# An encoder layer in split float32: the low parts of weights and modulated rows made by VectorE alone

## The chip, the cores and the metric

The kernel runs on one core of one Trainium2 chip. The metric is the device time of one execution in microseconds, and of several executions the median. The engines are TensorE (PE, with its weight loads as PEld), VectorE (DVE), ScalarE (ACT), GpSimd (POOL) and SyncE (SP, which here only issues DMAs).

## The reference

One encoder layer is computed for two independent sequences of 512 rows and 1024 columns (b = 0 and b = 1 below), with the same weights, all in float32:

```python
mod = silu(c) @ w_ada + b_ada                 # six vectors: sh1, sc1, g1, sh2, sc2, g2
h = rms_norm(x, norm1_g) * (1 + sc1) + sh1
q_a, k_a, v_a, q_r, k_r, v_r, g_r = split(h @ w_in)
o_a = windowed_attention(q_a, k_a, v_a, sink)  # 8 heads, 2 key heads, |t - s| <= 128, ALiBi, a sink logit
o_r = bidirectional_retention(q_r, k_r, v_r, g_r)   # 4 heads of 128, forward and backward decay, gated
x = x + g1 * (concat(o_a, o_r) @ w_out)
h = rms_norm(x, norm2_g) * (1 + sc2) + sh2
x = x + g2 * (square(relu(h @ w_mlp1)) @ w_mlp2)
y = rms_norm(x, final_g)
```

w_in has 2816 columns (512 q_a, 128 k_a, 128 v_a, and four times 512 for q_r, k_r, v_r, g_r), w_mlp1 4096.

## The kernel before, in words

**Split products.** To keep float32 accuracy with TensorE's faster format (fp32r), each operand is split in a high part (a cast to fp32r, made by ScalarE) and a low part (the operand less its high part, a subtraction). A product is then three matmuls (`mm3`, lines 128 to 130): high x high, high x low, low x high. A low part is needed for the second or third of these only, so a little later than the high part. Names: `raw_..` is a weight as loaded, `wh_..` and `wl_..` are its high and low part; the suffix says which: rv (the retention's values, four units of 256 rows of the weight), rq, rk, rg (retention queries, keys and gates, one unit for each head), wo (the output projection, eight units). `h` is a modulated, transposed row block of the normed input, with both parts in one tile, `hm` the same before the split.

**The sequence.** The front (to about 75 us) makes the modulation of the first norm and the first six column blocks of the input projection for sequence 0. Then sequence 0's retention projections run unit by unit, mixed with its attention blocks (names `psc` scores, `st` scores after the bias, `negm` and `den` softmax statistics, `ppt` and `pt` transposed weights, `po` outputs; the two digits behind a name are the head group and the block of 128 queries) and then with its retention heads (`prs`, `rsf`, `rsc` scores, `py` and `ryt` output, `pyn`, `ryn`, `pyb` the per-head norm, `dtab` the decay table). From 175 us `norm_x1` loads, norms (`rv_x`, `rr_x`, `x`) and modulates the rows of sequence 1, and the same projections follow for it, from the split weights that sequence 0 has stored in DRAM (`keep_unit`, `kept_unit`): there no weight is split again. From about 415 us the output projection of sequence 0 runs with its own splits, then that of sequence 1 from the stored ones, and from about 520 us the MLP, in a scheme of seven products instead of eight. Beside all this, `ada_gate` and `ada_columns` build the other modulation vectors as running sums on VectorE (`adacc_g`, `adacc_c`), four units of weights each; the gates are written to DRAM by a DMA that GpSimd issues (`gates`).

**What sets the order.** A unit's `load` (a load on SP into `raw`, the cast on ACT, the subtraction) is issued one unit ahead of its use, and `between` mixes steps of attention, retention, norm and background into the matmuls. The order that comes out is then a scheduler's, engine by engine; at run time each engine works through its list strictly in that order and waits on semaphores. In the front the order is pinned as written; behind it, moving an instruction to another engine also moves others. SP's list has, for each unit of sequence 0, the stores of its high and low part, each of which waits for its part, and the load of a later unit behind them. `raw` has three buffers, the split weights four (two units).

**Who made the low parts.** In the front they are shared between DVE and GpSimd. Behind the front GpSimd makes those of all weight units (line 103 of `split_unit`, with `lo_engine`) and those of `h` for the odd column blocks of sequence 1 (line 328); DVE makes the rest: those of `h` for even blocks, of scores, transposed weights, projections and mixed outputs. GpSimd also computes the powers of the norms (`rr_x` line 306, `rrs` line 485) and issues the gates' stores (line 292).

Of the kernel before, what the change touches and what calls it, by code (L numbers as in the profile page):

```python
# [15 lines left out]
P = 128  # L16
# [3 lines left out]
KC = D // P  # L20
# [10 lines left out]
def trunk_kernel(ctx, tc, x0, x1, c0, c1, w_ada, b_ada, norm1_g, w_in, attn_sink, decay_f, decay_b,  # L31
                 w_out, norm2_g, w_mlp1, w_mlp2, final_g, y0, y1):
    nc = tc.nc
    xin = (x0[0], x1[0])
    yout = (y0[0], y1[0])
    w_ada, b_ada, w_in, w_out = w_ada[0], b_ada[0], w_in[0], w_out[0]
# [12 lines left out]
    def mm_bank(name):  # L49
        return psum.tile([P, 512], F32, tag="mm", name=name, bufs=3)  # L50
# [4 lines left out]
    def r4(name, dtype=F32R):  # L55
        return work.tile([P, 2, 512], dtype, tag="r4", name=name, bufs=N_R4)
# [4 lines left out]
    def f2(name, dtype=F32):  # L61
        return work.tile([P, 512], dtype, tag="f2", name=name, bufs=8)
# [7 lines left out]
    def f(ap):  # L70
        return ap.bitcast(F32)
# [14 lines left out]
    def raw_unit(src, name, spare=False):  # L86
        t = r4f(f"raw_{name}") if spare else work.tile([P, 1024], F32, tag="raw", name=f"raw_{name}", bufs=3)
        n = src.shape[1] * src.shape[2]
        nc.sync.dma_start(t[:, :n].rearrange("p (a n) -> p a n", n=src.shape[2]), src)
        return t  # L90

    def split_high(t, name, pool=None):
        if pool is spare_ws:
            w = [r4(f"w{s}_{name}").rearrange("p a n -> p (a n)") for s in "hl"]
        else:
            w = [(pool or work).tile([P, 1024], F32R, tag="ws", name=f"w{s}_{name}", bufs=4) for s in "hl"]
        nc.scalar.copy(w[0], t)
        return w

    def split_unit(src, name, lo_engine, pool=None):  # L100
        t = raw_unit(src, name)
        w = split_high(t, name, pool)
        lo_engine.tensor_sub(w[1], t, f(w[0]))  # L103
        return [x.rearrange("p (a n) -> p a n", n=src.shape[2]) for x in w]
# [4 lines left out]
    def keep_unit(key, w):  # L109
        d = kept[key] = tc.dram_tile((P, 2, 1024), F32, name=f"kept_{key}")  # L110
        for s in range(2):
            nc.sync.dma_start(d[:, s, :], f(w[s]).rearrange("p a n -> p (a n)"))

    def kept_unit(key, name, n, lows=None):
        w = []
        for s in range(2):
            pool, tag, bufs = ((work, "ws", 4), lows or (work, "raw", 3))[s]
            t = pool.tile([P, 1024], F32R, tag=tag, name=f"w{'hl'[s]}_{name}", bufs=bufs)
            nc.sync.dma_start(f(t), kept[key][:, s, :])
            w.append(t.rearrange("p (a n) -> p a n", n=n))  # L120
        return w

    def cols_unit(wt, k0, nk, col, n):
        return wt[k0 * P:(k0 + nk) * P, col:col + n].rearrange("(k p) n -> p k n", p=P)

    def mm3(ps, lhs, rhs, start, stop):

        nc.tensor.matmul(ps, lhs[0], rhs[0], start=start, stop=False)  # L128
        nc.tensor.matmul(ps, lhs[0], rhs[1], start=False, stop=False)  # L129
        nc.tensor.matmul(ps, lhs[1], rhs[0], start=False, stop=stop)  # L130
# [192 lines left out]
    def modulated(which, b, kc, src):  # L323
        dst = r4(f"h_{which}_{b}_{kc}")
        t = f2(f"hm_{which}_{b}_{kc}")
        nc.vector.tensor_scalar(t, src, mod_a[which][:, kc, b:b + 1], mod_s[which][:, kc, b:b + 1], ALU.mult, ALU.add)
        nc.scalar.copy(dst[:, 0, :], t)
        (nc.vector if kc % 2 == 0 or which == b == 0 else nc.gpsimd).tensor_sub(dst[:, 1, :], t, f(dst[:, 0, :]))
        return dst

    def split2(ps_, name):
# [305 lines left out]
    def proj_unit(hT, col, name, done):  # L637
        key = f"in{col}"

        def load():  # L640
            if hT is hT_of[1]:
                return kept_unit(key, name, P)
            return split_unit(cols_unit(w_in, 0, KC, col, P), name, nc.gpsimd)

        def use(w):
            bank = mm_bank(f"pj_{name}")
            for k in range(KC):
                mm3(bank, (w[0][:, k, :], w[1][:, k, :]), (hT[k][:, 0, :], hT[k][:, 1, :]), k == 0, k == KC - 1)
                if k == 3:
                    yield  # L650
            done(bank)
            yield
        return Unit(load, use, done, None if hT is hT_of[1] else lambda w: keep_unit(key, w))
# [34 lines left out]
    def ret_v_units(hT, b):  # L688

        banks = []  # L690

        def unit(kq):
            key = f"rv{kq}"

            def load():
                if b == 1:
                    return kept_unit(key, f"rv{b}_{kq}", 512)
                return split_unit(cols_unit(w_in, kq * 2, 2, 1792, 512), f"rv{b}_{kq}", nc.gpsimd)

            def use(w):  # L700
                if kq == 0:
                    banks.extend((mm_bank if t < 3 else aux_bank)(f"pj_rv{b}_{t}") for t in range(NT))
                for t in range(NT):
                    tsl = slice(t * P, (t + 1) * P)
                    for k in range(2):
                        kk = kq * 2 + k
                        mm3(banks[t], (hT[kk][:, 0, tsl], hT[kk][:, 1, tsl]), (w[0][:, k, :], w[1][:, k, :]),
                            kk == 0, kk == KC - 1)
                    if kq == 3:
                        ret_v[b].append(split2(banks[t], f"rv_{b}_{t}"))  # L710
                    if t == 1:
                        yield
                yield
            return Unit(load, use, None, (lambda w: keep_unit(key, w)) if b == 0 else None)
        return [unit(kq) for kq in range(4)]
# [20 lines left out]
    def out_units(b, late=None):  # L736
# [10 lines left out]
        def unit(hf, kq):  # L747
            hs = slice(hf * 512, (hf + 1) * 512)

            key = f"wo{hf}_{kq}"  # L750

            def load():
                if b == 1:
                    w = kept_unit(key, f"wo{b}_{hf}_{kq}", 512, (late, "ws2", 3))
                else:
                    w = split_unit(cols_unit(w_out, kq * 2, 2, hf * 512, 512), f"wo{b}_{hf}_{kq}", nc.gpsimd)
                if hf == 0:
                    ms = halves[kq] = []
                    for k in range(2):
                        m_ = r4(f"ms_{b}_{kq}_{k}")  # L760
                        nc.scalar.copy(m_[:, 0, :], mix[kq][:, k, :])  # L761
                        nc.vector.tensor_sub(m_[:, 1, :], mix[kq][:, k, :], f(m_[:, 0, :]))
                        ms.append(m_)
                if kq == 2:
                    gr[hf] = gate_row(0, b, hs)
                return w, halves[kq]

            def use(wm):
                w, ms = wm
                if kq == 0:  # L770
                    banks[hf] = [(mm_bank if t < 3 else aux_bank)(f"po_{b}_{hf}_{t}") for t in range(NT)]
                for t in range(NT):
                    tsl = slice(t * P, (t + 1) * P)
                    for k in range(2):
                        kk = kq * 2 + k
                        mm3(banks[hf][t], (ms[k][:, 0, tsl], ms[k][:, 1, tsl]), (w[0][:, k, :], w[1][:, k, :]),
                            kk == 0, kk == KC - 1)
                    if t == 1:
                        yield
                if kq == 3:  # L780
                    for t in range(NT):
                        if hf == 0:
                            x2[t] = x2_tile(t)
                            tc.keep_in_program_order(nc.sync.dma_start(x2[t], xin[b][t * P:(t + 1) * P, :]))
                        g_ = f2(f"go_{b}_{hf}_{t}")
                        nc.vector.tensor_tensor(g_, banks[hf][t], gr[hf], ALU.mult)
                        nc.vector.tensor_tensor(x2[t][:, hs], x2[t][:, hs], g_, ALU.add)

                    def squares():
                        for t in range(NT):  # L790
                            nc.scalar.activation(junk(f"jk2_{b}_{hf}_{t}")[:, :512], x2[t][:, hs], AF.Square,
                                                 accum_out=ss[t][:, hf:hf + 1])
                    if hf == 0:
                        later.append((clock[0] + 2, squares))
                    else:
                        halves["squares"] = squares
                yield
            return Unit(load, use, None, (lambda wm: keep_unit(key, wm[0])) if b == 0 else None)

        def norm2():  # L800
# [677 lines left out]
```

## Time and profile before

| | us |
|---|---|
| median of three runs | 1181.89 |
| the three runs | 1181.77 to 1184.57 |
| the profiled execution | 1184.46 |
| its span in the trace | 1182.7 |
| PE, DVE, ACT, POOL busy in it | 1117.8, 933.6, 493.9, 133.4 |

The profiled execution is 2.6 us above the median, and 1.8 us of it lie outside the span that the trace shows. Times in the trace are counted from the span's start. A matmul's recorded duration includes its way through the array, so consecutive ones overlap. "PEclk" is the share of full speed that TensorE's clock was granted. In the views, `out<-in` names what an instruction writes and reads, "x" how many of them; in a wait, the name ahead of the arrow waits for the one behind it, with the us in total, the times, and the longest.

### The profile page before, as it was taken

How to read it: one execution, taken by the hardware profiler on the slowest of the kernel's cores; microseconds unless marked ns; L12 is line 12 of the kernel's file. 1: busy time of each engine (PE TensorE's matmuls, PEld its weight loads, DVE VectorE, ACT ScalarE, POOL GpSimd, SP SyncE). 2: the span in 40 equal slices, each digit the busy share in tenths (PEclk: the TensorE clock that was granted, in tenths of full speed). 3: DMA queues.
4: the chain of work that ended last, by engine and by line, in shares of the span. 5: the costliest groups of instructions: out<-in, count | busy, mean ns of one | idle time of the engine just before them, and what ended most of it. 6: DMA issues, size and time to landing. Idle time of an engine off the chain costs nothing.

```text
span 1182.7 us, 14508 instructions
## 1 busy us (share of the span) xinstructions
PE 1117.8 (95%) x5167; PEld 909.0 (77%) x5167; DVE 933.6 (79%) x1522; ACT 493.9 (42%) x846; POOL 133.4 (11%) x107
## 2 busy tenths in 40 slices
PE   5889899999999999999999999999999999999975
PEld 3667777777888878888878888888778888888854
DVE  4887978877887687598998778886686876968896
ACT  4446665433745234246333333333444432432341
POOL 3632223301000033100000000000000000000012
PEclk9999999989999999999999999999999999999988
DMA  9786557554545578951655455542767264363513
GB/s 286 232 270 222 194 186 264 198 198 160 184 160 174 179 257 325 334 186 62 208 175 179 156 175 188 166 160 98 259 221 266 80 200 147 123 215 126 195 36 142
DMA packets 124112, 224.36 MB, mean 190 GB/s; under 512 B 8501, under 2 KB 59781, under 8 KB 124041
## 3 DMA queue, kind: packets, MB, share of 16 engines
q1 hardware_dynamic: 111144, 217.14, 54.9%
q10 hardware_dynamic: 12544, 6.29, 1.8%
q8 instruction: 40, 0.66, 0.2%
q0 software_dynamic: 352, 0.03, 0.1%
q14 instruction: 32, 0.25, 0.1%
HBM read 152.36 MB, written 71.06 MB: 189 GB/s over the span
## 4 chain that ended last, share of the span: by engine, by line
PE 69%; DVE 12%; DMA 4%; issue 3%; ACT 3%; POOL 2%; DVEq 0%; POOLq 0%; ACTq 0%; SPq 0%
PE px_None L936 13%; PE x L1310 12%; PE py_None L936 9%; PE y L1310 9%; PE po L129 2%; PE po L128 2%; PE po L130 2%; PE ppt L422 1%; PE po L429 1%; DVE adacc_g L255 1%; DMA raw_ada_c<-in_w_ada_dram 1%; PE psc L396 1%; PE pj_rk L128 1%; PE pj_rk L130 1%; PE pj_rg L130 1%
## 5 line engine op out<-in xcount | busy, mean ns | idle before, releaser
L841 ACT CAST uc_0h<-ur 128x1024 fp32r<-128x1024 f32 x28 | 29.4, 1052 | 68.7 <-PE x L1310 38.1
L1310 PE MATMUL x<-wc_0l,uc_0h 128*128 128x512 f32 x128 | 51.0, 398 | 5.4 <-DVE wc_0l L842 5.4
L1310 PE MATMUL x<-wc_0h,uc_0h 128*128 128x512 f32 x128 | 50.8, 398 | 3.9 <-DVE acc L1356 3.2
L128 PE MATMUL po<-wh_wo,ms 128*128 128x512 f32 x128 | 51.0, 398 | 2.6 <-ACT ms L761 2.0
L1310 PE MATMUL x<-wc_1h,uc_1h 128*128 128x512 f32 x128 | 50.5, 396 | 2.3 <-ACT wc_1h L841 2.3
L129 PE MATMUL po<-wl_wo,ms 128*128 128x512 f32 x128 | 50.5, 395 | 0.7 <-POOL wl_wo L103 0.7
L1310 PE MATMUL x<-wc_1l,uc_1h 128*128 128x512 f32 x128 | 50.5, 394 | 0.5 <-DVE wc_1l L842 0.5
L1310 PE MATMUL x<-wc_0h,uc_0l 128*128 128x512 f32 x128 | 50.5, 395 | 0.0
L1310 PE MATMUL x<-wc_1h,uc_1l 128*128 128x512 f32 x128 | 50.5, 395 | 0.0
L842 DVE TENSOR_TENSOR uc_0l<-ur,uc_0h 128x1024 fp32r<-128x1024 f32 x28 | 34.2, 1221 | 20.1 <-ACT uc_0h L841 16.3
L130 PE MATMUL po<-wh_wo,ms 128*128 128x512 f32 x128 | 49.4, 390 | 0.0
L255 DVE SCALAR_TENSOR_TENSOR adacc_c<-raw_ada_c,cact,adacc_c 128x512 f32<-128x512 f32 x56 | 42.9, 800 | 7.2 <-DMA raw_ada_c<-in_w_ada_dram 6.2
L406 ACT ACTIVATE st<-st,negm 128x256 f32<-128x256 f32 (+1 forms) x64 | 35.2, 555 | 20.3 <-DVE negm L401 20.2
L841 ACT CAST wc_0h<-w 128x1024 fp32r<-128x1024 f32 x24 | 25.2, 1049 | 43.6 <-DVE w L1289 17.6
L841 ACT CAST wc_s4h<-raw_w 128x1024 fp32r<-128x1024 f32 x16 | 16.8, 1052 | 62.6 <-PE px_None L936 41.6
L255 DVE SCALAR_TENSOR_TENSOR adacc_g<-raw_ada_g,cact,adacc_g 128x512 f32<-128x512 f32 x56 | 42.2, 784 | 0.4 <-ACT adacc_g L253 0.3
L1365 POOL TENSOR_SCALAR msf<-ssf 128x1 f32<-128x1 f32 x8 | 4.3, 540 | 336.0 <-ACT jkf L1362 335.9
L842 DVE TENSOR_TENSOR wc_0l<-w,wc_0h 128x1024 fp32r<-128x1024 f32 x24 | 29.3, 1221 | 13.5 <-ACT wc_0h L841 13.4
L936 PE MATMUL py_None<-hch,wc_a 128*128 128x512 f32 x120 | 39.7, 390 | 0.1
L936 PE MATMUL px_None<-hch,wc_a 128*128 128x512 f32 x120 | 39.5, 390 | 0.0
L936 PE MATMUL px_None<-hch,wc_s 128*128 128x512 f32 x120 | 39.4, 389 | 0.0
L1310 PE MATMUL y<-wc_1l,uc_1h 128*128 128x512 f32 x96 | 37.5, 390 | 0.6 <-DVE wc_1l L842 0.6
(398 smaller groups left out, 3583.4 us busy)
## 6 DMA issues: line engine op xcount, KB each, us to landing
ur<-spill SPq DMA_DIRECT2D x56, 512.0 KB, 4.2
raw_w<-in_w_mlp_dram SPq DMA_DIRECT2D x32, 512.0 KB, 4.3
spill<-s SPq DMA_DIRECT2D x64, 256.0 KB, 4.2
w<-in_w_mlp_dram SPq DMA_DIRECT2D x32, 512.0 KB, 5.8
spill<-u SPq DMA_DIRECT2D x48, 256.0 KB, 2.3
raw_ada_g<-in_w_ada_dram SPq DMA_DIRECT2D x16, 512.0 KB, 4.4
raw_ada_c<-in_w_ada_dram SPq DMA_DIRECT2D x16, 512.0 KB, 4.2
raw_ada<-in_w_ada_dram SPq DMA_DIRECT2D x12, 512.0 KB, 8.9
```

The source lines that it names most:

```text
L128: nc.tensor.matmul(ps, lhs[0], rhs[0], start=start, stop=False)
L129: nc.tensor.matmul(ps, lhs[0], rhs[1], start=False, stop=False)
L130: nc.tensor.matmul(ps, lhs[1], rhs[0], start=False, stop=stop)
L255: nc.vector.scalar_tensor_tensor(acc[b], src, cb, acc[b], ALU.mult, ALU.add)
L396: nc.tensor.matmul(psc[:, :w], qs[hh][:, isl], k_[:, s, j0 * P:j1 * P], start=(s == 0), stop=(s == 1))
L406: nc.scalar.activation(st[hh][:, :w], st[hh][:, :w], AF.Exp, bias=negm[:, hh:hh + 1], scale=0.125, accum_out=den[:, hh:hh + 1])
L422: nc.tensor.transpose(pt[:, hh * P:(hh + 1) * P], st[hh][:, jj * P:(jj + 1) * P], ident)
L429: nc.tensor.matmul(po, va[:, j0 + jj, g].rearrange("p s e -> p (s e)"), pts[jj][:, s, :], start=(jj == 0 and s == 0), stop=(jj == nj - 1 a ...
L841: nc.scalar.copy(hi, src)
L842: nc.vector.tensor_sub(lo, src, f(hi))
L936: self.last = nc.tensor.matmul(bank[:, cs], x[:, k, :], y, start=first and k == 0 and i == 0, stop=last and k == 3 and i == 2, skip_group_ ...
L1310: nc.tensor.matmul(out, u[x][:, i % 2, ts_], w[y][:, i % 2, :], start=first and i == 0 and k == 0, stop=end and i == GP - 1 and k == 2, sk ...
```

## The change

All low parts that GpSimd made behind the front are made by VectorE: the operand `lo_engine` of three calls of `split_unit` is `nc.vector`, and the condition on line 328 goes. These are 4 rv, 12 rq, rk and rg, and 8 wo units of 128x1024, and four `h` of 128x512. GpSimd keeps the norms' powers and the gates' stores, and its share of the pinned front.

```diff
@@ def modulated
         nc.scalar.copy(dst[:, 0, :], t)
-        (nc.vector if kc % 2 == 0 or which == b == 0 else nc.gpsimd).tensor_sub(dst[:, 1, :], t, f(dst[:, 0, :]))
+        nc.vector.tensor_sub(dst[:, 1, :], t, f(dst[:, 0, :]))
@@ def proj_unit
-            return split_unit(cols_unit(w_in, 0, KC, col, P), name, nc.gpsimd)
+            return split_unit(cols_unit(w_in, 0, KC, col, P), name, nc.vector)
@@ def ret_v_units
-                return split_unit(cols_unit(w_in, kq * 2, 2, 1792, 512), f"rv{b}_{kq}", nc.gpsimd)
+                return split_unit(cols_unit(w_in, kq * 2, 2, 1792, 512), f"rv{b}_{kq}", nc.vector)
@@ def out_units
-                    w = split_unit(cols_unit(w_out, kq * 2, 2, hf * 512, 512), f"wo{b}_{hf}_{kq}", nc.gpsimd)
+                    w = split_unit(cols_unit(w_out, kq * 2, 2, hf * 512, 512), f"wo{b}_{hf}_{kq}", nc.vector)
```

The scheduler puts the moved subtractions into DVE's list and reorders around them; from the MLP on the lists are the same. Three places follow, each a piece of the difference (- before, + now).

On DVE, at the softmax of head group 0's last block (at about 127 us; `pt` are transposed weights of the block before, `adacc_g` running sums, `den` and `rden` the block's denominators):

```order
 L334 TENSOR_TENSOR pt_0_2_2_1248<-ppt_0_2_2_1243,pt_0_2_2_1248 128x512
-L255 SCALAR_TENSOR_TENSOR adacc_g_0_0_1054<-raw_ada_g_0_2_1459,cact,adacc_g_0_0_1054 128x512
+L255 SCALAR_TENSOR_TENSOR adacc_g_0_1_1055<-raw_ada_g_0_1_1251,cact,adacc_g_0_1_1055 128x512
+L103 TENSOR_TENSOR wl_rk_0_1260<-raw_rk_0_1257,wh_rk_0_1259 128x1024
 L409 TENSOR_TENSOR den_0_3_1196<-den_0_3_1196,es_0_3_1194 128x4
-L255 SCALAR_TENSOR_TENSOR adacc_g_0_1_1055<-raw_ada_g_0_2_1459,cact,adacc_g_0_1_1055 128x512
+L437 TENSOR_TENSOR mix_0_807<-po_0_2_1279,otmp_0_2_1286 64x2x128
 L411 RECIPROCAL rden_0_3_1203<-den_0_3_1196 128x4
```

The low part of the first key unit now stands ahead of the denominators, and two running sums of the next weights have moved further down.

On DVE, where the rows of sequence 1 are normed (at about 183 us; `rv_x` is the input of the power on GpSimd, `x` the scaled rows, `dl` and `dtab` the decay table of head 1):

```order
 L286 TENSOR_TENSOR adsp_0_0_1_1830<-adacc_g_0_0_1054,adsp_0_0_0_1829 128x512
+L103 TENSOR_TENSOR wl_rg_2_1942<-raw_rg_2_1939,wh_rg_2_1941 128x1024
 L304 TENSOR_SCALAR rv_x_0_1866<-ssq_0_1863 128x1
+L559 TENSOR_SCALAR dl_0_1_1895<-dl,nlb 128x896
 L321 TENSOR_SCALAR x_0_1855<-x_0_1855,rr_x_0_1868 128x1024
-L559 TENSOR_SCALAR dl_0_1_1895<-dl,nlb 128x896
+L304 TENSOR_SCALAR rv_x_1_1874<-ssq_1_1871 128x1
 L561 TENSOR_TENSOR dtab_1_1896<-dtab_1_1896,dl_0_1_1895 128x896
-L304 TENSOR_SCALAR rv_x_1_1874<-ssq_1_1871 128x1
 L321 TENSOR_SCALAR x_1_1857<-x_1_1857,rr_x_1_1876 128x1024
```

A gate unit's low part now stands ahead of the first tile's statistics, and the second tile's `rv_x` ahead of `dtab` instead of behind it.

On POOL, from the power of the last tile of sequence 1 to that of the first retention head's norm (190 to 213 us):

```order
 L306 TENSOR_TENSOR rr_x_3_1892<-rv_x_3_1890,neghalf 128x1
-L103 TENSOR_TENSOR wl_rq_3_2033<-raw_rq_3_2030,wh_rq_3_2032 128x1024
-L328 TENSOR_TENSOR h_1_1_2003<-hm_1_1_2004,h_1_1_2003 128x512
 L292 DMA gates<-adacc_g_0_0_1054 16x1x32
-L103 TENSOR_TENSOR wl_rk_3_2123<-raw_rk_3_2120,wh_rk_3_2122 128x1024
-L328 TENSOR_TENSOR h_1_3_2088<-hm_1_3_2089,h_1_3_2088 128x512
 L485 TENSOR_TENSOR rrs_0_2113<-rva_0_2111,neghalf 128x4
```

The gates' store and the power stand directly behind one another now. Elsewhere PE's list has some transposes and small products later among the projection's matmuls (the `pyn` of the first retention head five matmuls later, the `ppt` of the last attention block behind the rest of `pj_rg`), and SP's list has the store of `wh_rk` for head 2 ahead of the four loads of `x` instead of behind them.

## The prediction

> **What bounds the kernel now.** I read the page's head first, then the stages in which the moved instructions stand, and last what TensorE (PE) waits for in them.
>
> ```profile
> PE 1117.8 (95%) x5167; PEld 909.0 (77%) x5167; DVE 933.6 (79%) x1522; ACT 493.9 (42%) x846; POOL 133.4 (11%) x107
> ```
>
> PE is busy for 95% of the span, so time is to be had only where it stands still or runs at a low clock. The stage table (us, then busy time of PE, PEld, DVE, ACT, POOL, then PE's granted clock and DMA) gives the room of each engine:
>
> ```profile
> 68.00:112.00 44.00, 40.63 (x194) 31.77 (x192) 33.90 (x81) 26.72 (x56) 12.51 (x7) 1.00 0.77 247
> 112.00:165.00 53.00, 50.02 (x257) 41.08 (x256) 45.16 (x117) 35.92 (x87) 13.78 (x6) 1.00 0.63 203
> 165.00:245.00 80.00, 71.87 (x320) 56.89 (x319) 65.24 (x114) 36.87 (x66) 27.07 (x18) 0.94 0.65 217
> 415.00:480.00 65.00, 62.32 (x280) 51.13 (x279) 51.68 (x94) 24.30 (x41) 22.97 (x11) 0.97 0.83 289
> ```
>
> DVE is fullest in 112:165 (45.16 of 53, 85%) and has about a fifth free elsewhere. PE's waits from 68 to 245 us, and below the "..." those of 412 to 482:
>
> ```profile
> PE po L429 <- DVE pt L334: 3.0, 2, 1.8
> PE pyb L493 <- DVE ryn L488: 2.5, 1, 2.5
> PE px L312 <- DVE x L321: 2.0, 1, 2.0
> PE ppt L422 <- DVE st L416: 1.8, 1, 1.8
> PE pyn L476 <- ACT ryt L472: 1.8, 1, 1.8
> PE pj_rv L129 <- POOL wl_rv L103: 1.6, 1, 1.6
> PE first L128 <- ACT h L327: 1.0, 1, 1.0
> ...
> PE po L128 <- ACT ms L761: 2.0, 1, 2.0
> PE po L129 <- POOL wl_wo L103: 0.7, 1, 0.7
> ```
>
> Only two name GpSimd (1.6 and 0.7), yet GpSimd stands behind most of the others, as the change part shows. Two waits are also followed by a stretch at half clock:
>
> ```profile
> 190.60:194.00 3.40, 3.40 (x10) 2.62 (x10) 3.00 (x7) 3.00 (x7) 1.10 (x2) 0.53 1.02 386
> 238.40:245.20 6.80, 6.10 (x16) 4.63 (x17) 4.42 (x9) 0.62 (x1) 0.19 (x1) 0.51 0.38 124
> ```
>
> Half clock over 3.4 us of work is 1.7 us lost, over 6.8 us at most 3.4; these follow the waits for x and for ryn. The Trainium skill, page "TensorE: Matmul & The Clock Gate", section "Part 1: The HAM clock gate", puts the fall to half clock behind at least one idle window of about 3.4 us. Neither wait here is that long (2.0 and 2.5 us), so by the page both clock terms would drop out of the sum below and the gain would be 5.5 us and the time 1176, inside the range of my own case. The rows show the clock at 0.53 and 0.51 and decide: the terms stay.
>
> **The change, part by part.** 24 subtractions of 128x1024 (four wl_rv, twelve of wl_rq, wl_rk, wl_rg, eight wl_wo) and four of 128x512 (h) go from POOL to DVE. Their prices are in the trace on both engines, POOL first, then DVE (ns min/median/max):
>
> ```profile
> L103 POOL TENSOR_TENSOR wl_wo<-raw_wo,wh_wo x8: 2392/2402/2917, 420.8 to 468.8; 128x1024 fp32r<-128x1024 f32 x8
> L842 DVE TENSOR_TENSOR wc_0l<-w,wc_0h x24: 1216/1219/1226, 844.8 to 1143.8; 128x1024 fp32r<-128x1024 f32 x24
> L328 DVE TENSOR_TENSOR h<-hm,h x12: 679/692/2120, 24.1 to 226.3; 128x512 fp32r<-128x512 f32 x12
> ```
>
> DVE's bill is 24 x 1.22 + 4 x 0.69 = 32.0 us. What comes back is time in which DVE stands inside an instruction while a POOL subtraction runs. Five places show it; POOL's row stands ahead of DVE's:
>
> ```profile
> L401 DVE TENSOR_SCALAR negm<-mx x16: 157/166/2166, 94.2 to 360.1; 128x4 f32<-128x4 f32 x16
> L416 DVE TENSOR_SCALAR st<-st,rden x32: 336/403/2453, 99.6 to 364.2; 128x256 f32<-128x256 f32 x16, 128x384 f32<-128x384 f32 x16
> L561 DVE TENSOR_TENSOR dtab<-dtab,dl x4: 1062/1579/3171, 170.2 to 251.6; 128x896 f32<-128x896 f32 x4
> ...
> 74.40 2.60 POOL L103 TENSOR_TENSOR wl_rv<-raw_rv,wh_rv 128x1024 fp32r<-128x1024 f32 x1 [2.65 <-ACT wh_rv L97]
> 74.78 3.04 DVE L1024 TENSOR_TENSOR wil<-raw_wi,wih 128x768 fp32r<-128x768 f32 x1
> 121.72 2.40 POOL L103 TENSOR_TENSOR wl_rk<-raw_rk,wh_rk 128x1024 fp32r<-128x1024 f32 x1 [7.91 <-ACT wh_rk L97]
> 121.98 2.17 DVE L401 TENSOR_SCALAR negm<-mx 128x4 f32<-128x4 f32 x1
> 170.49 2.99 POOL L103 TENSOR_TENSOR wl_rq<-raw_rq,wh_rq 128x1024 fp32r<-128x1024 f32 x1 [6.88 <-ACT wh_rq L97]
> 171.18 2.72 DVE L416 TENSOR_SCALAR st<-st,rden 128x256 f32<-128x256 f32 x2
> 185.15 2.72 POOL L103 TENSOR_TENSOR wl_rg<-raw_rg,wh_rg 128x1024 fp32r<-128x1024 f32 x1 [0.92 <-ACT wh_rg L97]
> 185.65 3.17 DVE L561 TENSOR_TENSOR dtab<-dtab,dl 128x896 f32<-128x896 f32 x1
> 230.37 1.61 POOL L328 TENSOR_TENSOR h<-hm,h 128x512 fp32r<-128x512 f32 x1 [8.09 <-ACT h L327]
> 230.86 2.07 DVE L561 TENSOR_TENSOR dtab<-dtab,dl 128x896 f32<-128x896 f32 x1
> ```
>
> A negm of 128x4 needs 0.17 us and took 2.17; two st of 0.34 took 2.72; a dtab needs 1.06 and took 3.17 and 2.07; each ends as POOL's instruction ends. These stand straight ahead of the PE waits. The terms, each between 0 (the wait stays) and its full size:
>
> - First weights (wait 1.0): wil gives back 3.04 - 0.92 (three quarters of 1.22) = 2.1, and wl_rv's 1.22 now stands behind it. Net 0.9.
> - pj_rv for wl_rv (1.6): the cast wh_rv now stands earlier on ACT and the subtraction between the ks ones, and it is half as long. All 1.6.
> - po for pt (3.0): negm's 2.0 goes, but wl_rk's 1.22 enters the same softmax chain, ahead of den. I take half, 1.5.
> - ppt for st (1.8): 2.0 goes, 1.22 comes in front of den; and PE now has the rest of pj_rg ahead of these transposes. All 1.8.
> - px for x (2.0 + 1.7 of clock): x of the second tile waited on rv_x, queued behind the 3.17 us dtab. rv_x now stands ahead of dtab, against wl_rg's 1.22 further up and the x loads on SP, which now stand behind the store of wh_rk. I take 1.5 + 1.7 = 3.2.
> - pyn for ryt (1.8): ryt's buffer is freed by the store of the gates, issued on POOL behind two subtractions (next rows). The copy is done at 200.69, the issue came at 201.69: 1.0 earlier, and PE has five more matmuls ahead of pyn. All 1.8.
>
> ```profile
> 200.12 0.57 ACT L291 COPY adacc_g<-pg 1x512 f32<-1x512 f32 x1
> 201.69 0.55 POOL L292 DMA_DIRECT2D gates<-adacc_g  x1
> 207.44 0.59 ACT L472 COPY ryt<-py 128x512 f32<-128x512 f32 x1 [1.98 <-DMA gates<-adacc_g]
> ```
>
> - pyb for ryn (2.5 + up to 3.4 of clock): dtab's 1.0 goes and three running sums (adacc, 0.78 each by their group's mean on the page) move behind ryn, against wl_rg and two h (2.6) that come ahead of it; pyb's transposes stand among later matmuls. 2.0 + 2.0 = 4.0.
> - Output projection: the 0.7 for wl_wo goes, since PE has the L129 products later. The 2.0 for ms stays: it hangs on ACT's cast behind a late load.
>
> Together 0.9 + 1.6 + 1.5 + 1.8 + 3.2 + 1.8 + 4.0 + 0.7 = 15.5 us. At the upper end all of it goes: 1.0 + 1.6 + 3.0 + 1.8 + 3.7 + 1.8 + 5.9 + 0.7 = 19.5.
>
> Against it stands the new DVE work. In 112:165 it is 6 x 1.22 = 7.3 us. Of the relief there the rows show negm's 2.0, and the whole POOL time of 13.78 bounds it above. I take about 4, so DVE goes to 45.2 + 7.3 - 4 = 48.5 of a stage that is to shrink from 53 to 51: too full to hide everything. I charge 3 there, 1.3 in 68:112 (five subtractions, 6.1, against the stretched wil and some smaller ones), nothing in 165:245 and 415:480, where DVE has 15 and 13 us free, and 2 for a low part that now lies ahead of something urgent. That is 6.3, bounded by 0 and by the 32.0 of the bill. Loads: the next raw unit stands on SP behind the store of the low part, so a low part made later delays a load; PE needs it one unit ahead, and in most places the shorter instruction makes up for its place in DVE's queue. POOL keeps the powers (0.55 us each) and the gate stores, which only gain.
>
> Net 15.5 - 6.3 = 9.2, called 9. The profiled execution was 1184.46 (span 1182.7), so it would be 1175.5; the median of the runs shown is 1181.89, 2.6 lower, and the same 9 off gives **1173**.
>
> **The rivals.**
> 1. *Late casts hold DVE (slower).* On POOL a subtraction waited for its cast with nothing behind it. On DVE everything stands behind it.
>
> ```profile
> POOL wl_wo L103 <- ACT wh_wo L97: 30.8, 8, 5.4
> ACT wh_wo L97 <- DMA raw_wo<-in_w_out_dram: 12.0, 3, 6.4
> ```
>
> POOL waited 30.8 us over eight casts, of which ACT's own wait for loads is 12.0. If DVE comes to a subtraction before its cast is done, it idles. Decisive from 15.5 / 24 = 0.65 us of hold per subtraction; at 0.9 each it is 21.6 - 15.5 = +6, so 1188. For it: DVE's free fifth lets it arrive early. Against: DVE is 80% full and mostly late, and the subtraction stands a few instructions behind where its cast should end.
> 2. *DVE is the bound in the attention stretch, so nothing is left.* Eight low parts stand in softmax chains (ahead of den, negm or the pt), 9.8 us; if PE waits for each, and the place's relief is spent, 15.5 - 3.3 - 9.8 = 2.4 is left: 1179.5, and with a little of the first rival 1181. For it: 85% busy at 112:165. Against: PE's transposes there are placed later too. The Trainium skill, page "Perfetto Trace Analysis", section "Optimizing Scalar/DVE Operations", speaks for it: with a saturated DVE, handing work even to GPSIMD may make sense; it adds that the two share a port, so that it might not help.
> 3. *Everything comes back.* All 19.5, with 2 charged: 1164. For it: the waits all stand behind a stretched instruction. Against: po's and px's chains keep a new 1.22.
>
> That the work stays on POOL is excluded: no such row is left in its queue.
>
> **How the numbers follow.** Mine, 9 with its own range of 1166 to 1178: 0.56. The third: 0.12. The second: 0.19. The first: 0.13. Eight in ten takes mine, the second and most of the third: 1163 to 1183. Runs of this kernel spread over 0.24%, so about 0.3% (3.5 us) tells a change: faster means under 1178.3 (0.68), same up to 1185.4 (0.19), slower above (0.13).
>
> **What the profile would show.** Right: negm, st and dtab at their own 0.17, 0.34 and 1.06 without rows of 2 us; DVE's busy time up by only some 5 to 10 us, not 32; PE's waits for x, ryt and ryn short or gone, and the clock at 1.00 from 165 to 245. Wrong: DVE idle ahead of L103 for a cast wh, PE waits for pt or st of a microsecond each from 95 to 165, or half-clock stretches at new places.

## The result and the profile after

The changed kernel took 1161.86 us (median of 4 runs, 1160.54 to 1162.38) against 1181.83 us for the kernel before on the same chip (4 runs, 1179.67 to 1184.57): a ratio of 0.985, 95% interval 0.9826 to 0.9873. That is 20 us faster. The prediction had said 9 us and 1173, with a range that ends at 1163: the time lies just below the range. The profiled execution took 1161.89 us, so its trace stands for the median.

The head of its page:

```profile
span 1160.1 us, 14470 instructions
PE 1109.4 (96%) x5167; PEld 903.8 (78%) x5167; DVE 933.4 (80%) x1550; ACT 494.0 (43%) x846; POOL 69.0 (6%) x79
```

The number to stop at is DVE's. It runs 28 instructions more (1522 before), which by their own durations are 32.0 us of work. Successive DVE rows overlap by about 0.1 us, so in the busy time these 28 count for 28.6. Yet the busy time went from 933.6 to 933.4: the other 1522 take 28.8 us less of it, although nothing in them was changed. The rows say the same one by one. From 70 to 500 us the kernel before has DVE rows that are over 0.1 us longer than the same instruction's median in the changed kernel; the excess is 28.5 us in all, and each of these rows runs beside a GpSimd subtraction (27.3 us beside those that the change moves). The changed kernel has none there. "Busy" before had held that much time in which an instruction stood still.

The stages of the prediction's table, cut at the same places of the program (us, then busy time of PE, PEld, DVE, ACT, POOL, PE's clock and DMA):

```profile
68.00:107.60 39.60, 39.59 (x192) 32.26 (x190) 31.57 (x78) 25.50 (x55) 1.84 (x1) 0.98 0.82 267
107.60:158.20 50.60, 49.75 (x254) 41.08 (x253) 47.02 (x120) 36.44 (x87) 0.00 (x0) 1.00 0.67 220
158.20:227.50 69.30, 68.02 (x325) 54.25 (x324) 62.81 (x126) 37.72 (x66) 6.83 (x8) 1.00 0.71 240
398.40:461.70 63.30, 61.03 (x280) 50.07 (x279) 50.84 (x103) 24.47 (x41) 3.02 (x3) 1.00 0.86 297
```

They were 44.00, 53.00, 80.00 and 65.00 long, so they gave 4.4, 2.4, 10.7 and 1.7: together 19.2 of the 20. (The two spans differ by 22.6: the profiled execution of the kernel before lost 2.9 more behind 700 us, where the lists are the same.) The time for which PE stood still went from 3.4, 3.0, 8.1 and 2.7 us to 0.0, 0.9, 1.3 and 2.3. In the third stage the half clock went as well (0.94 before, 1.00 now), and in the last it is most of the gain: PE's busy time fell by 1.3 us there, with the clock up from 0.97 to 1.00.

PE's waits from 68 to 227.5 us are these four, and below the "..." the two of the output projection:

```profile
PE pj_rk L130 <- DVE wl_rk L103: 0.8, 1, 0.8
PE px L312 <- DVE rv_x L304: 0.5, 1, 0.5
PE px L312 <- DVE x L321: 0.4, 1, 0.4
PE pyb L493 <- DVE ryn L488: 0.3, 1, 0.3
...
PE po L128 <- ACT ms L761: 1.9, 1, 1.9
PE po L129 <- DVE wl_wo L103: 0.3, 1, 0.3
```

Before, the seven rows of that stretch came to 13.7 us. The waits for pt, st, ryt, wl_rv and h are gone. What is new is 0.8 us for a wl_rk.

DVE's three instructions whose longest cases the prediction quoted (ns min/median/max):

```profile
L401 DVE TENSOR_SCALAR negm<-mx x16: 149/162/170, 92.6 to 343.5; 128x4 f32<-128x4 f32 x16
L416 DVE TENSOR_SCALAR st<-st,rden x32: 345/382/424, 96.8 to 347.6; 128x256 f32<-128x256 f32 x16, 128x384 f32<-128x384 f32 x16
L561 DVE TENSOR_TENSOR dtab<-dtab,dl x4: 1079/1087/1092, 163.1 to 234.9; 128x896 f32<-128x896 f32 x4
```

The maxima were 2166, 2453 and 3171; now each lies within 12% of its median. The median didn't show it: for negm and st it was 166 and 403 before and is 162 and 382 now. It was the maximum beside it that told.

### The profile page after: what moved, and what is told of

It is laid out like the page before. It is cut to its first block, busy times and chain, and to the rows that moved or that the text cites. A ratio compares the mean times of both kernels' runs of the same rounds, so it can differ in the third digit from the quotient of the medians.

```text
span 1160.1 us, 14470 instructions
## 1 busy us (share of the span) xinstructions
PE 1109.4 (96%) x5167; PEld 903.8 (78%) x5167; DVE 933.4 (80%) x1550; ACT 494.0 (43%) x846; POOL 69.0 (6%) x79
## 4 chain that ended last, share of the span: by engine, by line
PE 75%; DVE 11%; DMA 5%; issue 3%; ACT 3%; POOL 2%; SPq 0%; ACTq 0%; DVEq 0%; POOLq 0%
PE px_None L936 12%; PE x L1310 12%; PE py_None L936 9%; PE y L1310 9%; PE po L129 2%; PE po L130 2%; PE po L128 2%; DMA raw_ada_g<-in_w_ada_dram 2%; PE po L429 1%; PE ppt L422 1%; PE psc L396 1%; PE pj_rq L129 1%; PE pj_rq L128 1%; PE pj_rv L128 1%; PE pj_rv L130 1%
## 5 line engine op out<-in xcount | busy, mean ns | idle before, releaser
L842 DVE TENSOR_TENSOR uc_0l<-ur,uc_0h 128x1024 fp32r<-128x1024 f32 x28 | 34.2, 1222 | 19.6 <-ACT uc_0h L841 15.9
L255 DVE SCALAR_TENSOR_TENSOR adacc_c<-raw_ada_c,cact,adacc_c 128x512 f32<-128x512 f32 x56 | 39.8, 748 | 6.7 <-DMA raw_ada_c<-in_w_ada_dram 5.7
L842 DVE TENSOR_TENSOR wc_0l<-w,wc_0h 128x1024 fp32r<-128x1024 f32 x24 | 29.3, 1221 | 13.5 <-ACT wc_0h L841 13.4
L1310 PE MATMUL y<-wc_0h,uc_0h 128*128 128x512 f32 x96 | 37.6, 392 | 0.0
```

What stands on the lines that cost most here:

```text
L255: nc.vector.scalar_tensor_tensor(acc[b], src, cb, acc[b], ALU.mult, ALU.add)
L842: nc.vector.tensor_sub(lo, src, f(hi))
L1310: nc.tensor.matmul(out, u[x][:, i % 2, ts_], w[y][:, i % 2, :], start=first and i == 0 and k == 0, stop=end and i == GP - 1 and k == 2, sk ...
```

## Experiments

Two theories share the credit for a lighter GpSimd. **The hold**: while GpSimd runs a subtraction that reads SBUF (the memory on the chip in which the engines' tiles lie), DVE stands still inside instructions such as negm, st and dtab. **The queue**: GpSimd's powers and its stores of the gates stood behind subtractions in its own list. A third question is the price of the new work on DVE, for which the prediction charged 6.3 us. Ratios are to the kernel before on the same chip, with their 95% intervals. Added lines shift the line numbers in some rows: L103 stays, and L416 is L421 in the first experiment; the tile names identify them.

**1. The hold brought back.** On top of the change GpSimd repeats each of the 24 weight subtractions, in two halves, into a tile that nobody reads. The lists of PE, DVE, ACT and SP are those of the changed kernel.

```diff
         lo_engine.tensor_sub(w[1], t, f(w[0]))
+        for c in range(2):
+            cs = slice(c * 512, (c + 1) * 512)
+            nc.gpsimd.tensor_sub(idle_t, t[:, cs], f(w[0])[:, cs])
```

> The changed kernel, and beside each of the 24 weight subtractions on VectorE GpSimd makes the same subtraction once more, in two halves of 128x512, into a scratch tile that nobody reads. The orders of TensorE, VectorE, ScalarE and the DMAs are the changed kernel's, row for row. Theory HOLD (the gain came because VectorE no longer stands still while GpSimd reads SBUF): rows of 1.5 to 3 us come back on negm, st, dtab and the like, VectorE's busy time rises by 15 to 25 us, and 10 us or more of the 20 are lost again: 1171 to 1181. Rival ORDER (the gain came from the half as long low part and the new order of the lists, which are both kept here): 1160 to 1164. Rival QUEUE (powers and gate stores stood behind subtractions in GpSimd's list): 1164 to 1167, and the same in the run with iota.

1185.93 us (1184.75 to 1187.27), ratio 1.0042 (1.0027 to 1.0057): the whole gain is gone, and a little more, some 24 us above the changed kernel and beyond the 1171 to 1181 that was expected. The new order and the half as long low part are both still there, so ORDER alone does not make the gain. Its page head, then from its timeline two st of DVE and the pair of GpSimd's instructions beside them, and its largest PE waits from 68 to 485 us:

```profile
PE 1117.0 (94%) x5167; PEld 905.5 (77%) x5167; DVE 963.0 (81%) x1550; ACT 494.3 (42%) x846; POOL 144.6 (12%) x127
```

```profile
121.73 1.82 DVE L421 TENSOR_SCALAR st<-st,rden 128x384 f32<-128x384 f32 x2
```

```profile
122.05 2.65 POOL L106 TENSOR_TENSOR idle_t<-raw_rk,wh_rk 128x512 bf16<-128x512 f32 x2 [6.67 <-ACT wh_rk L97]
```

```profile
PE ppt L427 <- ACT st L419: 3.6, 2, 2.0
PE ppt L427 <- DVE st L421: 3.0, 4, 0.8
PE px L317 <- DVE rv_x L309: 2.9, 2, 2.3
PE po L134 <- DVE wl_wo L103: 2.0, 1, 2.0
PE po L133 <- ACT ms L766: 1.9, 1, 1.9
PE pyb L498 <- DVE ryn L493: 1.5, 2, 1.4
```

DVE runs the same 1550 instructions and takes 963.0 instead of 933.4, so 29.6 us of pure hold from 75.6 us of GpSimd's work (144.6 - 69.0). Two st that need 0.8 together took 1.82 under a pair of GpSimd's instructions. Waits for st and ryn are back by name, and px waits again, now for rv_x; the wait for pt is not. GpSimd also keeps `raw` longer here, but PE gains no wait for a load by that, and ACT's casts of wo wait 7.8 us for theirs, against 10.2 in the changed kernel. In the stretch of the program that is 107.6:158.2 above DVE is now nearly full:

```profile
111.60:169.70 58.10, 52.16 (x254) 41.94 (x253) 55.45 (x122) 36.99 (x88) 16.14 (x12) 0.98 0.63 200
```

It is busy for 55.45 of 58.10 us, 95%.

**2. The queue without the hold.** At the same 24 places GpSimd does one tiny copy, which makes it wait as the subtraction did, and four iotas, instructions that write a pattern and read nothing.

```diff
         lo_engine.tensor_sub(w[1], t, f(w[0]))
+        nc.gpsimd.tensor_copy(idle_t[:, 0:1], f(w[0])[:, 0:1])
+        for c in range(4):
+            nc.gpsimd.iota(idle_t, pattern=[[1, 512]], ...)
```

> The changed kernel, and at the same 24 places GpSimd makes one copy of 128x1 from the high part and then four iota of 128x512 into a scratch tile: GpSimd is occupied for about as long, but hardly reads SBUF. HOLD by reads alone: VectorE's two-input instructions keep their durations, 1160 to 1165. HOLD by any use of GpSimd's port: tensor_scalar rows like negm and st are stretched as before, 1165 to 1175. QUEUE: as much lost as in the run with the extra subtractions.

1164.93 us (1163.64 to 1165.98), ratio 0.9863 (0.9849 to 0.9878). GpSimd is nearly as full as in the first experiment, at 137.7 us against 144.6. By the medians this costs 3.1 us and by the ratios 1.5, and the interval overlaps the changed kernel's, so the times alone don't settle it. In the trace equal matmuls end up 3.0 us later than in the changed kernel, and 2.2 of that come at one place, the wait for x below.

```profile
L106 POOL IOTA idle_t<- 128x512 bf16 x96 | 54.5, 567 | 6.6
```

```profile
PE px L317 <- DVE x L326: 2.1, 1, 2.1
PE pj_rk L135 <- DVE wl_rk L103: 0.8, 1, 0.8
```

That wait of 2.1 is back because x waits 2.27 us for a power that stands behind three iotas in GpSimd's list. (49 of DVE's 1550 rows stand in another order in this run, all from 182 us on and so behind that wait.) So both theories hold, and their sizes are apart: about 3 us for the queue and, if the queue costs the same in the first experiment, some 21 of its 24 for the hold. The Trainium skill, page "SBUF — State Buffer", section "Who interferes with whom", says that a DVE instruction with two SBUF inputs contends with a GpSimd instruction that reads SBUF and not with one that only writes it. The two experiments agree: rsc and ms, which have two SBUF inputs, took 4.2 and 5.4 us more in the first than in the changed kernel, and no more in this one. The sentence does not cover st, negm and dl, which read one SBUF tile and at most a value for each row: they took 9.6 us more in the first experiment, and under iota st, negm and x still took 2.1 more. DVE's whole busy time rose by 29.6 us with reads and by 0.7 without.

**3. Twice the new work on DVE.** Each of the 24 subtractions runs twice on DVE.

```diff
         lo_engine.tensor_sub(w[1], t, f(w[0]))
+        lo_engine.tensor_sub(w[1], t, f(w[0]))
```

> The changed kernel with each of the 24 weight subtractions made twice on VectorE: 24 x 1.22 = 29.3 us more work there and nothing given back. The prediction's debit (6.3 of 32.0 us shown on TensorE) would put it at 1162 + 6 = 1168. If VectorE's work beside the matmuls is free as long as it has room: 1162 to 1164. If VectorE is the bound of the attention stretch: 6 x 1.22 in 112 to 165 us and more elsewhere shows, 1170 to 1180.

1175.52 us (1173.11 to 1180.81, 10 runs), ratio 0.9965 (0.9949 to 0.998). The second 29.3 us cost about 14. (In this run and the next the scheduler moved other rows too, some 80 and 60 of DVE's, so a part of their difference can be order.) Its largest PE waits and the two attention stages at the same places of the program:

```profile
PE pyb L494 <- DVE ryn L489: 3.4, 1, 3.4
PE pj_rq L131 <- DVE wl_rq L104: 2.9, 1, 2.9
PE po L130 <- DVE wl_wo L104: 2.6, 2, 2.4
```

```profile
110.50:168.80 58.30, 54.01 (x266) 44.52 (x265) 53.45 (x126) 37.63 (x89) 0.00 (x0) 0.97 0.61 194
168.80:241.70 72.90, 68.31 (x318) 53.84 (x317) 67.77 (x129) 36.30 (x65) 8.47 (x8) 0.98 0.65 218
```

DVE is at 92% and 93% in them. In the changed kernel it was already at 93% and 91%, with PE standing still for only 0.9 and 1.3 us; with more work the share stays and the stage grows (50.6 to 58.3). Two half-clock stretches of 3.4 us that the changed kernel does not have (from 149.90 and 218.16 us) are 3.4 of the 14 us.

**4. The new work taken off DVE.** The 24 subtractions are left out; GpSimd writes zeros into the low parts in their place, which reads nothing.

```diff
-        lo_engine.tensor_sub(w[1], t, f(w[0]))
+        if pool is None:
+            nc.gpsimd.memset(f(w[1]), 0.0)
+        else:
+            lo_engine.tensor_sub(w[1], t, f(w[0]))
```

The condition takes all 24 units.

> Leaves out the 24 weight subtractions behind the front: GpSimd writes zeros into the low parts instead, an instruction that reads nothing. Neither the hold nor VectorE's 24 x 1.22 = 29.3 us are there. The distance to the changed kernel (1162) is what VectorE's new work costs. The prediction's debit of 6.3 us: 1155 to 1157. Work that was free where it now stands: 1160 to 1163. If the second half of the bill is as dear as the doubling was (13.7 of 29.3 us): 1147 to 1150.

1161.62 us (1160.79 to 1166.08), ratio 0.9845 (0.9825 to 0.9865): the changed kernel's own time.

```profile
PE 1108.5 (96%) x5167; PEld 903.9 (78%) x5167; DVE 911.0 (79%) x1526; ACT 494.9 (43%) x846; POOL 91.5 (8%) x103
```

DVE lost subtractions that count for 26.5 us of its busy time in the changed kernel and is 22.4 less busy, so the memsets stretch the rest by some 4. That stretch might hide a small price, and so might the other order. PE's own rows give the bound: in the changed kernel its waits that name DVE in the four stages come to 2.3 us, and it stands still for 4.4 in all, of which 1.9 are the wait for ms. The new work costs between 0 and about 2 us, not 6.3.

**5. One part at a time.** Four kernels move only one of the four kinds, the other calls keep GpSimd: the four h; the four wl_rv; the twelve of wl_rq, wl_rk and wl_rg; the eight wl_wo. For the third the edit is, against the kernel before:

```diff
-            return split_unit(cols_unit(w_in, 0, KC, col, P), name, nc.gpsimd)
+            return split_unit(cols_unit(w_in, 0, KC, col, P), name, nc.vector)
```

> Only the four h of 128x512 go to VectorE, the weights stay on GpSimd. By the shifts of the trace the stage from 165 to 245 us gave most; of its holds 1.6 us stand on h (dtab at 230.86 us) and one on rva at 211.5. HOLD: 1 to 4 us of gain, 1177 to 1180. If most of the stage's gain hung on the gate store behind h in GpSimd's list: 4 to 6 us.

> Only the four units of the retention's values go to VectorE. The changed kernel's TensorE is 4.4 us earlier at 112 us than the one before (median shift of equal matmuls), all of it by these. Additive parts: 3 to 5 us of gain, 1176 to 1178. If the earlier softmax is lost again behind the holds of the next units: 0 to 2 us.

> Only the twelve units of retention queries, keys and gates go to VectorE. Shifts of the trace between 112 us and 260 us: 12 us, h included. Additive parts: 8 to 12 us of gain, 1169 to 1173. If the parts only pay together (one remaining hold on a critical row costs as much as several): 3 to 7 us.

> Only the eight units of the output projection go to VectorE. In the trace the stage from 415 to 480 us gave 1.7 to 2.6 us of the 20, though VectorE was held there for about 10 us. Parts that add up: 1.5 to 3 us of gain, 1177.5 to 1179. A hold shows on TensorE only where TensorE is about to use what VectorE makes next, so that much hold gives little time here. If each held microsecond were worth as much as in the run with the extra subtractions (24 us for 30): 8 us, 1172.

| moved alone | us | ratio (95%) | gain, us |
|---|---|---|---|
| h | 1177.50 | 0.9977 (0.9964 to 0.999) | 3.0 |
| wl_rv | 1175.83 | 0.9961 (0.9946 to 0.9976) | 4.7 |
| wl_rq, wl_rk, wl_rg | 1167.35 | 0.9885 (0.987 to 0.99) | 13.2 |
| wl_wo | 1177.45 | 0.9983 (0.9969 to 0.9998) | 2.5 |

The sum is 23.4 against 20.0 and 19.6 together (two measurements): additive within the noise, since each gain is known to about 1.5 us. Three came out as expected for parts that add up; the projections (third row) gained more than the 8 to 12 us expected. Per subtraction that is 0.75, 1.2, 1.1 and 0.3 us. No part was a loss, and those in the fullest stretch of DVE (in the third row) were not either.

**6. The same move in the front.** The change left 13 low parts of the front on GpSimd (six wl_ada, seven wil). Three kernels move them too: all; only the first seven (three wl_ada, four wil, up to about 45 us); only the six wl_ada.

```diff
-    def split_wi(kc, engine=nc.vector, low=nc.gpsimd):
+    def split_wi(kc, engine=nc.vector, low=nc.vector):
-    low_pair(2, 1, 1, nc.gpsimd)
+    low_pair(2, 1, 1, nc.vector)
...
```

> The changed kernel with the front's low parts (six wl_ada of 128x1024, seven wil of 128x768) on VectorE too: 6 x 1.22 + 7 x 0.92 = 13.8 us more work there before 80 us, while GpSimd's own 13 subtractions (29 us in the trace) stop holding VectorE. HOLD: VectorE's busy time is about even and the front ends 2 to 5 us earlier: 1157 to 1160. If the front waits for loads: 1161 to 1163. If VectorE's pinned list is full there: later by up to 5 us, 1164 to 1167.

> The changed kernel with the first seven low parts of the front (three wl_ada, four wil, up to about 45 us) on VectorE too; the later six stay on GpSimd. With all thirteen TensorE was 1.7 us earlier at 45 us and then lost ground until 85 us. Early lead kept: 1159.5 to 1161. Lead lost at the next late load: 1161.5 to 1163.

> The changed kernel with the front's six wl_ada on VectorE too, the seven wil on GpSimd: 7.3 us more work on VectorE against about 8 us of hold that goes. HOLD alone counts: 1158 to 1162. VectorE full in the front, so that a subtraction in its list costs its whole length where TensorE waits for it: 1164 to 1168.

> The changed kernel itself once more, beside the three above on the same chip: 0.983 to 0.987 of the time before.

All 13: 1170.69 us (1166.48 to 1171.92), ratio 0.9901 (0.9879 to 0.9923). The first seven: 1163.16, 0.9871 (0.9853 to 0.989). The six: 1164.10, 0.9874 (0.9856 to 0.9893). The changed kernel again, on the chip of these two: 1160.40 (1158.53 to 1161.38), 0.9841 (0.9823 to 0.986). So no version beats the changed kernel. The full move loses 6 us by the ratios and 9 by the medians, more than the up to 5 that were expected at worst; for the other two the intervals overlap the changed kernel's. From 24 to 45 us the front stands so in the changed kernel, and below it with all 13 moved:

```profile
24.00:45.00 21.00, 17.83 (x94) 12.01 (x95) 19.41 (x27) 8.80 (x13) 12.13 (x6) 1.00 0.82 273
24.00:45.00 21.00, 20.08 (x114) 13.62 (x112) 18.43 (x34) 10.01 (x15) 0.00 (x0) 1.00 0.86 284
```

Here the move helps, although DVE was busy for 19.41 of 21.00: it makes 34 instructions instead of 27 in less busy time, and PE works for 20.1 us instead of 17.8. The loss comes behind it. With all 13 moved, these are PE's longest waits behind its first tables, and below them the rows of 45 to 65 and 65 to 92 us:

```profile
PE pmt L229 <- ACT mr L221: 7.0, 3, 3.9
PE pj_rv L128 <- ACT vt_a L353: 3.0, 1, 3.0
```

```profile
45.00:65.00 20.00, 16.02 (x82) 11.44 (x79) 12.93 (x28) 7.76 (x14) 0.00 (x0) 0.91 0.65 183
65.00:92.00 27.00, 21.71 (x89) 16.18 (x90) 16.35 (x38) 11.69 (x20) 0.00 (x0) 0.84 1.03 323
```

The wait for mr grew from 2.5 us to 7.0, and the clock fell from 1.00 to 0.91 over 45:65 and from 0.94 to 0.84 over 65:92, which is 20 x 0.09 + 27 x 0.10 = 4.5 us. Equal matmuls stand 0.4 us later at 40 to 60 us (median), 3.0 at 60 to 80 and 8.2 from 80 on, so nearly all of the loss lies there. DVE is busy for only 65% and 61% of these two rows, so it is not DVE's being full that loses; what makes mr late was not separated.

## Why the prediction was wrong, step by step

**The mechanism and the direction were right.** GpSimd's reading holds DVE, and the waits of PE stood behind held instructions that mostly don't name GpSimd. Experiment 1 brings waits for st, ryn and px back with nothing added but GpSimd's instructions. One reading of the rows was off: it has all five held rows end with POOL's instruction. The negm does (124.15 against 124.12), but the wil ends 0.8 us later and the two dtab 0.95, nearly their own lengths. So a held row does not run slowly; it stands until POOL's instruction is done and then takes about its own time.

**The step that failed is the debit of 6.3** "against it stands the new DVE work". It measured 0 to 2 (experiment 4 and the waits after). Half of it, the 3 charged in 112:165, did not fail by the load that was read there: the prediction had 7.3 of new work against a relief of "about 4", so 48.5 us in a stage of 51, and DVE came out at 47.0 in 50.6 (the new subtractions count for 6.6, all other rows for 40.5 instead of 45.2). It failed by the conclusion, "too full to hide everything": with DVE busy for 93% of the stage PE waits there 0.8 us. The 1.3 in 68:112 measured 0.0, since PE stands still for 0.01 of its 39.60 us now, and the 2 for a low part ahead of something urgent 1.1 (the waits for wl_rk and wl_wo). Over the whole kernel the relief is 28.8 us, as large as the new work's 28.6, where the five places that were looked at show 9 or so. Hold and new work are also not worth the same per microsecond. A hold falls on whatever DVE is at, urgent or not: 24 us of time for 29.6 of hold in experiment 1. The new work stands where the scheduler put it: 29.3 us for 0 to 2, and in experiment 3 the next 29.3 for 14. That the difference is DVE's room is argued, not shown.

**The terms of the sum**, 15.5 predicted with an upper end of 19.5:

- First weights 0.9, pj_rv 1.6, ppt 1.8, pyn 1.8: no such waits are left. Right in kind, but the first two, 2.5 together, are too small for their stage, which gave 4.4; the wl_rv alone gave 4.7.
- po for pt, 1.5 of 3.0, since a wl_rk now stands ahead of den: mis-sized. The whole 3.0 went, 0.8 came for wl_rk itself.
- px for x, 3.2: 0.9 of the 2.0 is left and the half clock is gone, so 1.1 + 1.7 = 2.8.
- pyb for ryn, 4.0: mis-sized. 2.2 of 2.5 went and all of the half clock, up to 3.4: 5.6 at most.
- Output projection, 0.7: mis-sized. Of the wait for wl_wo 0.3 is left, and the stage gave 1.7, wl_wo alone 2.5 (interval 0.2 to 3.7). The wait for ms stayed at 1.9 as predicted, but the half clock that had followed it before went, which the sum had left out (why it went is in the last section, and it is luck):

```profile
422.70:426.10 3.40, 2.70 (x7) 2.15 (x7) 3.40 (x5) 1.53 (x3) 0.69 (x1) 0.53 0.47 111
```

```profile
404.00:414.00 10.00, 8.08 (x34) 6.39 (x35) 9.80 (x15) 4.64 (x9) 0.00 (x0) 1.00 0.73 234
```

The first row is of before, the second of the same place after. With these the terms add up to 0.9 + 1.6 + 2.2 + 1.8 + 2.8 + 1.8 + 5.6 + 1.7 = 18.4, against the 19.2 of the stages: the list of waits was good, and nearly all of it came back. That the two sums lie so close is partly luck: stage by stage it is 2.5 against 4.4, 2.2 against 2.4, 12.0 against 10.7 and 1.7 against 1.7. The 18.4 already has the new waits in it, so it stands against the net forecast of 9.2: 2.9 more by the terms, 6.3 by the debit. The last 1.6 to the measured 20 are in no term.

**The gates' store** did what the prediction said. The copy and the issue stand directly behind one another now, and the row of ryt behind them has no wait:

```profile
190.11 0.57 ACT L291 COPY adacc_g<-pg 1x512 f32<-1x512 f32 x1
190.97 0.55 POOL L292 DMA_DIRECT2D gates<-adacc_g  x1 [6.34 <-ACT adacc_g L291]
```

**What the profile was to show**: negm, st and dtab at their own durations came out; "busy time up by only some 5 to 10" did not, it was 0; the waits for x, ryt and ryn and the clock of 1.00 came out.

**The rivals.** The first (casts that hold DVE) needed 0.65 us per subtraction. DVE's waits for a cast at L103, the groups of the trace:

```profile
DVE wl_rv L103 <- ACT wh_rv L97: 0.9, 1, 0.9
DVE wl_rg L103 <- ACT wh_rg L97: 0.6, 1, 0.6
DVE wl_wo L103 <- ACT wh_wo L97: 0.4, 1, 0.4
```

With 0.2 for wl_rk that is 2.1 us over 24, under 0.1 each. The second (DVE the bound) was close: DVE is 93% busy in 107.6:158.2, and with twice the new work (experiment 3) the stage grows. The third (everything comes back, 1164) is what happened, at 0.12 too low a chance. Its objection, a wl_rk or wl_rg in the chains of po and px, was worth at most the 0.8 + 0.9 that are left there.

**The Trainium skill's two rules.** By the page "TensorE: Matmul & The Clock Gate", section "Part 1: The HAM clock gate", the half-clock stretches would have had no part in this, since the waits were shorter than its window of about 3.4 us. Here they went when the waits of 2.0 and 2.5 us went, and in experiment 2 a wait of 2.1 us for x is followed by one again, from 182.76 to 186.18 us:

```profile
182.76:186.18 3.42, 3.42 (x10) 2.64 (x9) 2.11 (x6) 2.88 (x5) 1.10 (x2) 0.50 0.32 130
```

The measurement decides. The length fits, for the half-clock stretches here last 3.41 us or twice that; that the window has to be idle does not, as the last section shows. The Trainium skill's page "Perfetto Trace Analysis", section "Optimizing Scalar/DVE Operations", says that handing work from a full DVE to GpSimd may make sense and warns that the two share a port. The warning decided here: DVE at 80% to 93% took 29 us of work for 0 to 2 us of time, and GpSimd doing it cost 20.

## What to carry to other kernels

Look at the longest case of each DVE instruction beside its median, and lay GpSimd's rows over the long ones: GpSimd's own busy time (11% here) says nothing of what it costs. When work goes from an engine that disturbs to the one that it disturbs, count the disturbance that goes over all held rows, not over the few in sight: here it was as large as the new work, which then cost next to nothing. A busy share does not tell what more work will cost: DVE at 93% still let PE run, the next 29 us cost half their length, and in the front thirteen more lost 6 to 9 us while DVE was under 70% busy where the loss arose.

## What was not expected of the hardware

- A GpSimd that only writes (iota) is nearly harmless to DVE: 68.7 us more of GpSimd's work, 54.5 of them iota, left DVE's busy time at 934.1 (933.4). Memsets of 128x1024 were less so, some 4 us of stretch from 24 of about 0.95.
- The hold's size: 75.6 us of GpSimd's two-input work stretched DVE by 29.6, and the 64.4 us that GpSimd is less busy after the change (133.4 - 69.0) had stretched it by 28.8. It is less than the whole overlap, since not every DVE instruction is held. In the kernel before all six rsc that ran beside a moved subtraction were held, by 6.2 us together. Of the 40 pt, which read one input (ppt) from PSUM, the memory that matmuls write, six ran beside one, and none is long:

```profile
L334 DVE TENSOR_TENSOR pt<-ppt,pt x40: 675/682/692, 101.7 to 367.2; 128x512 fp32r<-128x512 f32 x40
```

- The half clock is not settled by the length of one wait: one of 1.9 us (ms, after) was followed by none, one of 2.1 (x, experiment 2) was. The traces show what sets it apart. But for the ends of a run, every half-clock stretch lasts 3.41 or 6.83 us, and their starts lie whole multiples of 3.41 us apart (190.81, 238.60 and 422.92 us in the kernel before), so the clock changes on a grid of 3.41 us. These are the slots of the grid just ahead of three half-clock stretches, for x, ryn and ms in the kernel before, and ahead of that in experiment 2:

```profile
187.40:190.81 3.41, 1.40 (x8) 0.93 (x7) 2.23 (x3) 1.96 (x4) 1.03 (x2) 1.00 0.06 26
235.18:238.60 3.42, 1.45 (x7) 0.87 (x5) 2.52 (x6) 0.61 (x2) 1.47 (x1) 1.00 1.02 305
419.50:422.91 3.41, 1.26 (x7) 0.61 (x5) 3.41 (x4) 3.33 (x6) 2.15 (x1) 1.00 0.38 154
179.35:182.76 3.41, 1.31 (x7) 0.78 (x6) 1.52 (x2) 0.00 (x0) 2.23 (x5) 1.00 0.68 280
```

PE's matmuls fill 37% to 42% of them. The wait for ms in the changed kernel, from 403.65 to 405.59, lies across a border of the grid and leaves both of its slots fuller:

```profile
400.78:404.20 3.42, 2.87 (x15) 2.19 (x13) 3.42 (x8) 1.27 (x2) 0.00 (x0) 1.00 0.12 43
404.20:407.61 3.41, 2.02 (x9) 1.68 (x10) 3.21 (x6) 3.38 (x7) 0.00 (x0) 1.00 0.82 268
```

Over the 14 traces, from 20 us on, every full-clock slot that PE's matmuls filled by less than 43% was followed by half clock, and none that they filled by more than 54%; in between it went either way. So where a wait falls on the grid counts beside its length, and a slot at half clock costs 1.7 us on top of the wait. The wait for ms is nearly as long as before (1.9 against 2.0 us) and lost its half clock by its place.
